# Layer 1 of a two-layer hybrid backbone: attention scores, value products and LRU gates on the whole 128x128 array

## The chip, the cores and the metric

The kernel runs on one core of one Trainium2 chip. The metric is the device time of one execution in microseconds (us). Engines are named as in the profile: PE (TensorE, matrix products), PEld (its weight loads), DVE (VectorE), ACT (ScalarE), POOL (GpSimd) and SP (SyncE, which here only issues DMAs). Each engine carries out its own list of instructions in order, and waits on semaphores for the others.

## The reference, cut to what matters

The model has two layers for 512 latent tokens and 256 context tokens. The change lies in the token mixing of layer 1, which has an RG-LRU over 512 channels and a neighbourhood attention of 8 heads of 64 channels.

```python
def rglru(u_pre, gate_pre, conv_w, conv_b, gate_w, gate_b, lam, h0):
    u = conv(u_pre) + conv_b
    gates = jnp.einsum('btnc,zgncd->btzgnd', u.reshape(B, T, LRU_BLOCKS, LRU_BW), gate_w)   # 8 blocks of 64 x 64
    gates = jax.nn.sigmoid((gates.reshape(B, T, 2, 2, W) + gate_b).astype(jnp.float32))
    rg, ig = gates[:, :, :, 0], gates[:, :, :, 1]
    log_a = -LRU_C * rg * jax.nn.softplus(-lam.astype(jnp.float32))
    a = jnp.exp(log_a)
    xin = jnp.sqrt(-jnp.expm1(2 * log_a)) * ig * u[:, :, None, :]
    _, h = lax.associative_scan(_linear_combine, (a, xin), axis=time)      # z = 0 forwards, z = 1 backwards
    y = h[0] + jnp.flip(h[1], 1)
    return y.astype(u_pre.dtype) * jax.nn.gelu(gate_pre), h[:, :, -1]
```

The attention takes, for each head and each block of 16 columns of the 8 x 64 grid, the scores of 128 queries against 256 local and 256 context keys, adds a bias and a mask to the local ones, and multiplies the softmax with the values. After the mixing come the output projection, a gated residual add, and an MLP.

## The kernel before, in words

Everything is held with channels on partitions and tokens along the free dimension. A dense product is made by `gemm`: a weight tile `w` comes by DMA on SP's queue, ACT casts its high part `wh`, POOL (at times DVE) subtracts the low part `wl`, and PE makes `wh*xh + wh*xl + wl*xh` into a PSUM tile `psg` of 128 x 512; such operands are of the type fp32r. Products of plain f32 operands are called by `mm` too; each of them has two records in the trace.

Layer 1's mixing runs over i = 0 to 3, each time `na(i)` (two heads of the attention, on partitions 0 to 63 and 64 to 127) and `lru(i)` (128 channels, which are two blocks of 64). The code is written in that order; a scheduler then sets the order of every engine's list, so products of `lru(i)` stand between those of `na(i)` and of `na(i+1)`.

- `na(p)`: three tiles of the input projection give the queries `qn`, keys `kl` and values. For each column block n and each head q, scores go to `pss` (2 buffers), DVE adds the bias `mb` and takes the maximum, ACT makes the exponential `sl` with its sum, DVE normalizes it, PE transposes it to `pst`, ACT copies that to `pT`, and PE makes the value product `pso` (1 buffer). The results gather in `ax`, which `split_x` turns into the high and low parts `yh`, `yl` of rows 2p+1.
- `lru(i)`: two tiles of the input projection, a convolution to `u`, then for each direction z and gate g the gate products to `psl` (1 buffer) for 256 and for 512 tokens, and their tanh on ACT. Behind the gates of a direction: Exp to `a`, a tanh, the square of `a` on POOL (`a2`), two products on DVE, Sqrt on ACT, a product on POOL, the scans on DVE (256 and 512 tokens). The sum of both directions is multiplied by the gelu branch on POOL and split into rows 2i of `yh`, `yl`.
- Tiles of the same `tag` in the pool `pl` share one buffer: `a0` and `a1` hold `a` of the two directions, `a2` the square and, earlier, the gelu's work tile.

After the four iterations `out_proj(1, 0, res, Y, 0, 6, ...)` makes 8 tiles from rows 0 to 5 of `yh`, `yl` (so it needs `lru(0)` to `lru(2)` and `na(0)` to `na(2)`), and `out_halves` makes the part of rows 6 and 7 (`lru(3)` and `na(3)`), for 256 tokens at a time. The MLP follows.

Of the kernel before, what the change touches and what calls it, by code (L numbers as in the profile page):

```python
# [117 lines left out]
def hybrid_kernel(ctx: ExitStack, tc: tile.TileContext, A, out):  # L118
# [36 lines left out]
    # conditioning: modulation columns of half the channels for pairs of indices, a generator over weight tiles  # L155
# [33 lines left out]
    def ada_first(q, pa, psa, tag):  # L189
        """Shift and scale of the first norm for a quarter of the channels."""  # L190
        ps = psa.tile([P, P], F32, tag=tag, name=nm("psada"))
        for k in range(NK):
            if k % 2 == 0:
                w = pa.tile([P, 2, 512], F32, tag="adaw", name=nm("adaw"))
                nc.sync.dma_start(w, A["ada_0"][q, k // 2])
            for j in range(4):
                mm(ps[32 * j:32 * j + 32, :], sc[:, k, :], w[:, k % 2, P * j:P * j + P], k == 0, k == NK - 1)
        rows = pa.tile([P, P], F32, tag="rows", name=nm("rows"), bufs=1)
        nc.vector.tensor_copy(rows, ps)
        pt = psa.tile([P, P], F32, tag=tag, name=nm("pst"))  # L200
        nc.tensor.transpose(pt, rows, ident)
        src = pt.rearrange("p (i t r) -> p i t r", i=2, t=2)
        for i in range(2):
            o = 8 * i + 2 * q
            bias = cols[:, COLS["ada_b"][0] + o:COLS["ada_b"][0] + o + 2]
            for cnd in range(2):
                nc.vector.scalar_tensor_tensor(mod[:, 0, o:o + 2, cnd], src[:, i, :, cnd], float(i), bias, op0=ALU.add, op1=ALU.add)
# [11 lines left out]
    def split_w(ap, both, pool=None):  # L219
        """High and low part of a weight tile; the low part takes turns between GpSimd and VectorE where both are free."""  # L220
        m = ap.shape[1]
        n = m if pool else D
        pool = pool or (wide[0] if wcount[0] % 3 == 2 else None) or wp
        wpool = wide[0] if wide[0] is not None and pool is wide[0] else wp
        w = wpool.tile([P, D], F32, tag="w", bufs=3 if wpool is wp else None, name=nm("w"))[:, 0:m]
        nc.sync.dma_start(w, ap)
        wh = pool.tile([P, n], F32R, tag="wh", name=nm("wh"))[:, 0:m]
        nc.scalar.copy(wh, w)  # L228
        wl = pool.tile([P, n], F32R, tag="wl", name=nm("wl"))[:, 0:m]
        wcount[0] += 1  # L230
        eng = nc.vector if (2, 0, 3, 1)[wcount[0] % 4] < both else nc.gpsimd
        eng.tensor_tensor(wl, w, wh.bitcast(F32), op=ALU.subtract)  # L232
        return wh, wl

    def gemm(ap, xs, psp, both=0, k0=0, k1=NK, x0=0):
        """One output tile [P, n] for each (high, low, n) in xs, three single-pass products per contraction tile."""
        w = split_w(ap[:, P * k0:P * k1], both)
        res = [gemm_w(w, x, psp, x0) for x in xs]
        for _ in range(bg[1]):
            next(bg[0], None)  # L240
        return res
# [12 lines left out]
    def halves(x):  # L254
        """The two halves of the tokens of an operand or a residual."""
        n = x[2] if isinstance(x, tuple) else x.shape[2]
        sl = (slice(0, n // 2), slice(n // 2, n))
        return [(x[0][:, :, a], x[1][:, :, a], n // 2) for a in sl] if isinstance(x, tuple) else [x[:, :, a] for a in sl]

    def gemm_group(ws, ps, xs):  # L260
        """Several output tiles with the contraction outermost, for an input that is still being made."""
        for k in range(NK):
            for (wh, wl), row in zip(ws, ps):
                for (xh, xl, _), p_ in zip(xs, row):
                    for a, (w, x_) in enumerate(((wh, xh), (wh, xl), (wl, xh))):
                        mm(p_, w[:, P * k:P * k + P], x_[:, k, :], k == 0 and a == 0, k == NK - 1 and a == 2)
# [5 lines left out]
    class Stats:  # L272
        """Sums of squares of every token, gathered tile by tile, and 1/rms on every partition."""
# [55 lines left out]
    def out_proj(layer, cnd, res, x, k0, k1, psp, both, stats=None, x0=None):  # L329
        """Part of the contraction of an output projection, a generator over weight tiles (yields their time on TensorE)."""  # L330
        for m in range(NK):
            add_gated(res[:, m, :], gemm(A["out_w"][layer, m], [x], psp, both, k0, k1, k0 if x0 is None else x0)[0], cnd, m, layer, 2)
            if stats:
                stats.add(res[:, m, :])
            yield x[2] / 512 * 0.65 * (k1 - k0)

    def out_halves(layer, res, x, k0, ws, psp, stats):
        """The last part of an output projection for one half of the tokens after the other."""
# [6 lines left out]
    def mlp(layer, cnd, n, res, FC, psp, side, both, rb, G, stats=None, done=None):  # L345
        us = n / 512 * 5.2
        with ExitStack() as st:
# [39 lines left out]
            if done:  # L387
                # the end by halves of the tokens, so that the first leaves while the second is made
# [8 lines left out]
    # ================= layer 0: modulated norm =================  # L397
# [37 lines left out]
    # derived per-channel columns  # L435
# [29 lines left out]
    # scratch in DRAM  # L465
# [104 lines left out]
    def mlstm_head(h):  # L570
# [32 lines left out]
        # scores, shared by both directions  # L603
# [204 lines left out]
    # ================= RWKV: chunked recurrence, both directions in step =================  # L808
# [4 lines left out]
    def add_set():  # L813
        """Tiles of every other chunk."""
        sets.append(st_r.enter_context(tc.tile_pool(name=f"set{len(sets)}", bufs=1)))
# [12 lines left out]
    def pre(s, X):  # L828
        """Everything of a chunk that does not need the state."""
# [23 lines left out]
        # inverses of the 16 x 16 diagonal blocks, one per partition  # L853
# [14 lines left out]
        # the keys by token  # L868
# [20 lines left out]
        # merge to 32 x 32 blocks, one per group of 32 partitions  # L889
# [19 lines left out]
        # merge to 64 x 64: only the block off the diagonal is new  # L909
# [69 lines left out]
    def rwkv_norm(y):  # L979
        """Head norm of some chunks [P, groups, chunks x pairs, 64], in place."""  # L980
# [13 lines left out]
    def rwkv_norms(s):  # L994
        """Head norm of the chunks that are complete after a step."""
# [6 lines left out]
    def rwkv_gate(si, dst, po, psp):  # L1002
        """Bonus and gate of a stream; dst(pair) is their place."""
# [11 lines left out]
    # ================= work that fills TensorE beside the recurrence =================  # L1015
# [3 lines left out]
    def lat_mlstm(res):  # L1019
        """The mLSTM part of the latents' output projection."""  # L1020
# [11 lines left out]
    def ctx_mlstm():  # L1032
        """The mLSTM part of the context's output projection."""
# [31 lines left out]
    def pull(gen, us):  # L1065
        """Emit units of gen worth us more microseconds of TensorE."""
# [74 lines left out]
    # ================= layer 0: latents =================  # L1141
# [34 lines left out]
    # ================= layer 1 =================  # L1176
# [23 lines left out]
    gw = pl.tile([P, 2, 2, 4, 64], F32, name="gw")  # L1200
    nc.scalar.dma_start(gw, A["gate_w"])
# [6 lines left out]
    def lru(i):  # L1208
# [21 lines left out]
        AA, XX = [], []  # L1230
        for z in range(2):
            th = []
            for g_ in range(2):
                t_ = pl.tile([P, T], F32, tag=f"t{g_}{z}", name=nm("th"))
                for off, n, _ in SEGS:
                    pq = psm.tile([P, n], F32, tag="l", name=nm("psl"))
                    for q in range(2):
                        mm(pq[hs_[q], :], gw[hs_[q], z, g_, i, :], u_[hs_[q], off:off + n])
                    nc.scalar.activation(t_[:, off:off + n], pq, AF.Tanh,
                                         bias=DV["lgb"][:, 8 * z + 4 * g_ + i:8 * z + 4 * g_ + i + 1], scale=0.5)  # L1240
                th.append(t_)
            tr, ti = th
# [32 lines left out]
    def na(p):  # L1275
        qn = pl2.tile([P, NB, 8, 16], F32, tag="qn", name=nm("qn"))
        pq, = gemm(A["od_in"][8 + p], XL, psg4)
        nc.scalar.activation(qn.rearrange("p n r c -> p r n c")[:, ::-1, :, ::-1], pq.rearrange("p (r n c) -> p r n c", r=8, n=NB),
                             AF.Copy, scale=0.125)
# [17 lines left out]
        # bias of the window, and what lies outside of it  # L1297
# [12 lines left out]
        ax = pl.tile([P, LT], F32, tag="ax", name=nm("ax"))  # L1310
        for n in range(NB):
            po_ = psm.tile([P, P], F32, tag="o", name=nm("pso"))
            for q in range(2):
                ps = psm.tile([P, 512], F32, tag="s", bufs=2, name=nm("pss"))
                qs = qn[hs_[q], n].rearrange("p r c -> p (r c)")
                s3 = ps[:, 0:256].rearrange("p (r c) -> p r c", r=8)
                mm(s3, qs, kl[hs_[q]].rearrange("p (r c) -> p r c", r=8)[:, :, BAND[n]:BAND[n] + 32])
                mm(ps[:, 256:512], qs, kc[hs_[q], :])
# [12 lines left out]
                for j in range(4):  # L1331
                    jv = 2 * n + j if j < 2 else 6 + j
                    mm(po_[hs_[q], :], vt_[:, jv, hs_[q]], pT[:, j, :], j == 0, j == 3)
            nc.vector.tensor_copy(ax.rearrange("p (r n c) -> p r n c", r=8, n=NB)[:, :, n, :],
                                  po_.rearrange("p (r c) -> p r c", r=8)[:, ::-1, ::-1])
        split_x(yh[:, 2 * p + 1, :], yl[:, 2 * p + 1, :], ax)
# [48 lines left out]
def _ktile(w, mt):  # L1385
    """[K, M] -> [M/mt][128][K/128 * mt], each tile's rows contiguous."""
# [83 lines left out]
```

## Time and profile before

| | us |
|---|---|
| three runs | 2079.46, 2080.81, 2088.39 |
| median | 2080.81 |
| span of the profiled execution, first to last instruction | 2084.8 |
| PE busy in the span | 1973.1 (95%) |
| mean granted clock of PE | 0.971 |

The profiled execution is one more execution of the program; of it the span is known, and no time around it is listed. The 95% are an average over stages. Matmuls are pipelined and a record's end is modelled, so a record of 0.39 us can have its successor 0.23 us behind it: what a matmul costs is read from the distance between starts. The stage of the change lasts from 1430.82 us (first query product of `na(0)`) to 1694.09 us (first product of `out_halves`).

### The profile page before, as it was taken

How to read it: one execution, taken by the hardware profiler on the slowest of the kernel's cores; microseconds unless marked ns; L12 is line 12 of the kernel's file. 1: busy time of each engine (PE TensorE's matmuls, PEld its weight loads, DVE VectorE, ACT ScalarE, POOL GpSimd, SP SyncE). 2: the span in 40 equal slices, each digit the busy share in tenths (PEclk: the TensorE clock that was granted, in tenths of full speed). 3: DMA queues.
4: the chain of work that ended last, by engine and by line, in shares of the span. 5: the costliest groups of instructions: out<-in, count | busy, mean ns of one | idle time of the engine just before them, and what ended most of it. 6: DMA issues, size and time to landing. Idle time of an engine off the chain costs nothing. (4 is left out here: it accounts for less than half of the span.)

```text
span 2084.8 us, 36853 instructions
## 1 busy us (share of the span) xinstructions
PE 1973.1 (95%) x14924; PEld 1599.6 (77%) x14924; DVE 1084.0 (52%) x2087; ACT 874.0 (42%) x1441; POOL 833.9 (40%) x561
## 2 busy tenths in 40 slices
PE   6999998889887999999999999999999999999998
PEld 4787776667676889888588888888666687888887
DVE  6754545767868666776551221253666663122122
ACT  5443445445533444443342332443665644233232
POOL 1455545233322222223144444435454454444444
PEclk9999999999888999999999999999999999999999
DMA  8355657554585555444633233335211122332332
GB/s 319 96 176 200 208 195 228 147 154 116 162 236 147 131 160 160 135 133 163 198 88 104 92 102 93 90 109 154 61 51 33 56 74 82 100 98 94 91 96 77
DMA packets 177595, 271.63 MB, mean 130 GB/s; under 512 B 75601, under 2 KB 114129, under 8 KB 177425
## 3 DMA queue, kind: packets, MB, share of 16 engines
q1 hardware_dynamic: 172368, 263.76, 42.0%
q10 hardware_dynamic: 5056, 5.51, 0.8%
q8 instruction: 118, 1.93, 0.4%
q14 instruction: 53, 0.43, 0.1%
HBM read 244.06 MB, written 25.17 MB: 129 GB/s over the span
## 5 line engine op out<-in xcount | busy, mean ns | idle before, releaser
L232 POOL TENSOR_TENSOR wl<-w,wh 128x1024 fp32r<-128x1024 f32 (+3 forms) x252 | 575.6, 2287 | 872.8 <-PE psg L134 425.2
L228 ACT CAST wh<-w 128x1024 fp32r<-128x1024 f32 (+3 forms) x319 | 313.5, 985 | 544.8 <-PE psg L134 463.2
L134 PE MATMUL psg<-xh,wh 128*128 128x512 f32 (+1 forms) x1440 | 503.2, 364 | 15.6 <-DVE k L699 3.1
L134 PE MATMUL psg<-xl,wh 128*128 128x512 f32 (+1 forms) x1440 | 502.1, 360 | 0.6 <-DVE xl L324 0.3
L134 PEld LDWEIGHTS psg<-xh,wh 128*128 128x128 f32 x1440 | 274.6, 192 | 76.9 <-issue 24.4
L134 PE MATMUL psg<-xh,wl 128*128 128x512 f32 (+1 forms) x1440 | 329.6, 359 | 0.0
L134 PEld LDWEIGHTS psg<-xl,wh 128*128 128x128 f32 x1440 | 276.4, 192 | 51.0 <-issue 10.2
L134 PEld LDWEIGHTS psg<-xh,wl 128*128 128x128 f32 x1440 | 242.7, 191 | 45.9 <-issue 10.5
L134 PE MATMUL psg<-hh,wh 128*128 128x512 f32 (+1 forms) x800 | 268.2, 352 | 3.7 <-DVE r L372 1.9
L134 PE MATMUL psg<-hl,wh 128*128 128x512 f32 (+1 forms) x800 | 270.8, 352 | 0.9 <-DVE hl L270 0.9
L327 DVE SCALAR_TENSOR_TENSOR res_l<-psg,mod,res_l 128x512 f32<-128x512 f32 (+1 forms) x108 | 74.3, 689 | 282.5 <-PE psg L134 282.4
L134 PEld LDWEIGHTS psg<-hh,wh 128*128 128x128 f32 x800 | 152.0, 190 | 25.6 <-DVE r L372 2.2
L134 PEld LDWEIGHTS psg<-hl,wh 128*128 128x128 f32 x800 | 152.3, 190 | 22.6 <-DVE hl L270 1.3
L134 PE MATMUL psg<-hh,wl 128*128 128x512 f32 (+1 forms) x800 | 166.0, 349 | 0.0
L134 PEld LDWEIGHTS psg<-hh,wl 128*128 128x128 f32 x800 | 131.7, 189 | 20.5
L372 DVE TENSOR_SCALAR r<-psg 128x512 f32<-128x512 f32 (+1 forms) x96 | 57.4, 599 | 171.0 <-PE psg L134 170.9
L270 DVE TENSOR_TENSOR hl<-r,hh 128x512 fp32r<-128x512 f32 (+1 forms) x96 | 88.1, 921 | 85.7 <-ACT hh L269 85.6
L373 ACT ACTIVATE r<-r 128x512 f32<-128x512 f32 (+1 forms) x96 | 53.5, 559 | 120.9 <-DVE r L372 120.9
L232 DVE TENSOR_TENSOR wl<-w,wh 128x1024 fp32r<-128x1024 f32 (+1 forms) x67 | 83.3, 1243 | 27.6 <-ACT wh L228 18.2
L134 PE MATMUL psada<-adaw,sc 128*32 128x256 f32 (+1 forms) x896 | 69.2, 378 | 12.4 <-DMA adaw<-in_ada_w_dram 6.8
L878 DVE TENSOR_TENSOR tm<-M,Xi 64x15 f32<-64x15 f32 (+4 forms) x180 | 63.9, 355 | 17.9 <-DMA M<-dA 14.4
L269 ACT CAST hh<-r 128x512 fp32r<-128x512 f32 (+1 forms) x96 | 52.6, 550 | 2.9
(418 smaller groups left out, 2852.8 us busy)
## 6 DMA issues: line engine op xcount, KB each, us to landing
w<-in_w_dram SPq DMA_DIRECT2D x192, 512.0 KB, 3.7
adaw<-in_ada_w_dram SPq DMA_DIRECT2D x80, 512.0 KB, 4.9
w<-in_ev_in_dram SPq DMA_DIRECT2D x47, 512.0 KB, 4.0
w<-in_od_in_dram SPq DMA_DIRECT2D x32, 512.0 KB, 3.7
adaw<-in_ada_dram SPq DMA_DIRECT2D x16, 512.0 KB, 11.4
w<-in_out_w_dram SPq DMA_DIRECT2D x32, 256.0 KB, 2.9
bk<-bkD SPq DMA_DIRECT2D x12, 512.0 KB, 4.5
ar<-arD SPq DMA_DIRECT2D x12, 512.0 KB, 4.7
```

Of the source, the lines that this page charges most:

```text
L134: return nc.tensor.matmul(o, l, r, start=start, stop=stop, skip_group_check=shared, **kw)
L228: nc.scalar.copy(wh, w)
L232: eng.tensor_tensor(wl, w, wh.bitcast(F32), op=ALU.subtract)
L269: nc.scalar.copy(h, x)
L270: nc.vector.tensor_tensor(l, x, h.bitcast(F32), op=ALU.subtract)
L327: nc.vector.scalar_tensor_tensor(r_, ps, modcol(layer, idx, m, cnd), r_, op0=ALU.mult, op1=ALU.add)
L372: nc.vector.tensor_scalar(r_, ps, 0.0, None, op0=ALU.max)
L373: nc.scalar.activation(r_, r_, AF.Square)
L878: nc.vector.tensor_tensor(t_, M[:, m:16, j:j + 1].to_broadcast([64, n, m]), Xi[:, j:j + 1, 0:m].to_broadcast([64, n, m]), op=ALU.mult)
```

## The change

Three groups of products that used 64 rows or 64 columns of the array use all 128 x 128 of it.

- Scores: the queries of each head go into their own tile `qz[:, q]`, whose other 64 partitions are zero, and the product contracts over all 128 partitions of `kl` and of `kc`. `qz` is one buffer, zeroed once by POOL, where `qn` had two; ACT fills it in two instructions for two heads.
- Value products: all 128 columns of the values are multiplied with each head's `pT`, and the half that belongs to the head is read from `pso`. The tile `ax` is gone: ACT casts `yh` and DVE makes `yl` from `pso` directly, for each block and head apart (64 x 128 each).
- Gates: the two 64 x 64 blocks stand on the diagonal of a zeroed 128 x 128 weight. Weights and `u` are split into fp32r parts `gwh`, `gwl`, `uh`, `ul`, and each gate is three fp32r products. The weights come by two DMAs on ACT's queue in each `lru`. `uh` and `ul` take the buffers `a0` and `a1`. All eight gate products of an `lru` are written ahead of both directions' further work.

```diff
-    gw = pl.tile([P, 2, 2, 4, 64], F32, name="gw")
-    nc.scalar.dma_start(gw, A["gate_w"])
+    gw = pl.tile([P, 4, P], F32, name="gw")
+    gwh = pl.tile([P, 4, P], F32R, name="gwh")
+    gwl = pl.tile([P, 4, P], F32R, name="gwl")
+    nc.gpsimd.memset(gw, 0.0)
...
+    qz = pl.tile([P, 2, GW // 16, 8, 16], F32, name="qz")
+    nc.gpsimd.memset(qz, 0.0)
...
-        AA, XX = [], []
...
+        for q in range(2):
+            nc.scalar.dma_start(gw[hs_[q], :, hs_[q]].rearrange("p (z g) c -> p z g c", z=2), A["gate_w"][hs_[q], :, :, i, :])
+        nc.scalar.copy(gwh, gw)
+        nc.gpsimd.tensor_tensor(gwl, gw, gwh.bitcast(F32), op=ALU.subtract)
+        uh = pl.tile([P, T], F32R, tag="a0", name=nm("uh"))
+        ul = pl.tile([P, T], F32R, tag="a1", name=nm("ul"))
+        split_x(uh, ul, u_)
+        TH = []
         for z in range(2):
-            th = []
             for g_ in range(2):
                 t_ = pl.tile([P, T], F32, tag=f"t{g_}{z}", name=nm("th"))
                 for off, n, _ in SEGS:
                     pq = psm.tile([P, n], F32, tag="l", name=nm("psl"))
-                    for q in range(2):
-                        mm(pq[hs_[q], :], gw[hs_[q], z, g_, i, :], u_[hs_[q], off:off + n])
+                    for a, (w, x) in enumerate(((gwh, uh), (gwh, ul), (gwl, uh))):
+                        mm(pq, w[:, 2 * z + g_, :], x[:, off:off + n], a == 0, a == 2)
                     nc.scalar.activation(t_[:, off:off + n], pq, AF.Tanh,
                                          bias=DV["lgb"][:, 8 * z + 4 * g_ + i:8 * z + 4 * g_ + i + 1], scale=0.5)
-                th.append(t_)
-            tr, ti = th
+                TH.append(t_)
+        AA, XX = [], []
+        for z in range(2):
+            tr, ti = TH[2 * z:2 * z + 2]
...
-        qn = pl2.tile([P, NB, 8, 16], F32, tag="qn", name=nm("qn"))
         pq, = gemm(A["od_in"][8 + p], XL, psg4)
...
+        for q in range(2):
+            nc.scalar.activation(qz[hs_[q], q].rearrange("p n r c -> p r n c")[:, ::-1, :, ::-1],
+                                 pq[hs_[q]].rearrange("p (r n c) -> p r n c", r=8, n=NB), AF.Copy, scale=0.125)
...
-                qs = qn[hs_[q], n].rearrange("p r c -> p (r c)")
+                qs = qz[:, q, n].rearrange("p r c -> p (r c)")
                 s3 = ps[:, 0:256].rearrange("p (r c) -> p r c", r=8)
-                mm(s3, qs, kl[hs_[q]].rearrange("p (r c) -> p r c", r=8)[:, :, BAND[n]:BAND[n] + 32])
-                mm(ps[:, 256:512], qs, kc[hs_[q], :])
+                mm(s3, qs, kl.rearrange("p (r c) -> p r c", r=8)[:, :, BAND[n]:BAND[n] + 32])
+                mm(ps[:, 256:512], qs, kc)
...
-                    mm(po_[hs_[q], :], vt_[:, jv, hs_[q]], pT[:, j, :], j == 0, j == 3)
-            nc.vector.tensor_copy(ax.rearrange("p (r n c) -> p r n c", r=8, n=NB)[:, :, n, :],
-                                  po_.rearrange("p (r c) -> p r c", r=8)[:, ::-1, ::-1])
-        split_x(yh[:, 2 * p + 1, :], yl[:, 2 * p + 1, :], ax)
+                    mm(po_[:, q, :], vt_[:, jv, :], pT[:, j, :], j == 0, j == 3)
+                src = po_[hs_[q], q].rearrange("p (r c) -> p r c", r=8)[:, ::-1, ::-1]
+                h_, l_ = (y[hs_[q], 2 * p + 1].rearrange("p (r n c) -> p r n c", r=8, n=NB)[:, :, n, :] for y in (yh, yl))
+                nc.scalar.copy(h_, src)
+                nc.vector.tensor_tensor(l_, src, h_.bitcast(F32), op=ALU.subtract)
```

The scheduler makes new lists from this. Three places of them show what moves. In the names, `psl_` numbers rise with the order in which the gate products are written; tiles `psg_16885` and above are those of the output projection.

PE's list of before, where the last `lru` begins (its first gate product is `psl_16795`) and the output projection starts (`psg_16889`):

```order
L134 MATMUL psl_16783<-u_16720,gw 64x512 x2
L1328 MATMUL pst_16652<-cst,sl_16648 128x128 x4
L134 MATMUL pso_16597<-pT_16634,vt_16479 64x128 x4
L1328 MATMUL pst_16673<-cst,sl_16669 128x128 x4
L134 MATMUL psl_16795<-u_16720,gw 64x256 x2
L134 MATMUL pso_16641<-pT_16657,vt_16479 64x128 x4
L134 MATMUL psg_16889<-yh_14998,wh_16885 128x512
L134 MATMUL psg_16889<-yl_14999,wh_16885 128x512
```

PE's list of the change at the corresponding place, from the last gate product of `lru(2)` (`psl_16425`) to the first of `lru(3)` (`psl_16866`); eight products of the output projection stand in it, of which two are shown:

```order
L134 MATMUL psl_16425<-uh_16382,gwh 128x512
L134 MATMUL psl_16425<-ul_16383,gwh 128x512
L134 MATMUL psl_16425<-uh_16382,gwl 128x512
L134 MATMUL pso_16681<-pT_16697,vt_16558 128x128 x4
L1341 MATMUL pst_16762<-cst,sl_16758 128x128 x4
L134 MATMUL psg_16993<-yh_14998,wh_16989 128x512
L134 MATMUL psg_16993<-yl_14999,wh_16989 128x512
...
L134 MATMUL pso_16681<-pT_16720,vt_16558 128x128 x4
L134 MATMUL pso_16728<-pT_16744,vt_16558 128x128 x4
L134 MATMUL pso_16728<-pT_16767,vt_16558 128x128 x4
L134 MATMUL psl_16866<-uh_16861,gwh 128x256
L134 MATMUL psl_16866<-ul_16862,gwh 128x256
```

Before, five of the eight gate products of `lru(3)` (`psl_16770` to `psl_16795`) stood ahead of the output projection, and the projection's first tile ran on through rows 0 to 5 without a break. Now all eight stand behind its first eight products, which cover rows 0 to 3; row 4 is the output of `lru(2)`.

The last gate product of `lru(3)` in PE's list of before, inside the fourth tile of the output projection; four and five sixths of its eight tiles, 87 products, follow before the first one of `out_halves` (`psg_17115`):

```order
L134 MATMUL psg_16967<-yh_14998,wh_16963 128x512
L134 MATMUL psl_16808<-u_16720,gw 64x512 x2
L134 MATMUL psg_16967<-yl_14999,wh_16963 128x512
...
L134 MATMUL psg_17071<-yh_14998,wl_17069 128x512 x6
L134 MATMUL psg_17115<-yh_14998,wh_16837 128x256
```

The same place in the change (`psg_17175` is the last tile of the output projection, `psg_17219` and `psg_17229` the first two of `out_halves`):

```order
L134 MATMUL psl_16899<-uh_16861,gwh 128x256
L134 MATMUL psl_16899<-ul_16862,gwh 128x256
L134 MATMUL psl_16899<-uh_16861,gwl 128x256
L134 MATMUL psg_17175<-yh_14998,wl_17173 128x512 x4
L134 MATMUL psl_16904<-uh_16861,gwh 128x512
L134 MATMUL psl_16904<-ul_16862,gwh 128x512
L134 MATMUL psl_16904<-uh_16861,gwl 128x512
L134 MATMUL psg_17219<-yh_14998,wh_16941 128x256
L134 MATMUL psg_17229<-yh_14998,wh_16947 128x256
L134 MATMUL psg_17219<-yl_14999,wh_16941 128x256
```

The 87 products between the last gate product and `out_halves` have become none.

ACT's list of the change behind the last two gate products, up to the cast of `lru(3)`'s output that `out_halves` reads (`th_16865`, `th_16876` are the tanhs of direction 0, `th_16887`, `th_16898` of direction 1):

```order
L1251 ACTIVATE th_16898<-psl_16899,der 128x256
L1259 ACTIVATE a_16916<-th_16887,der 128x768
L1251 ACTIVATE th_16898<-psl_16904,der 128x512
L1259 ACTIVATE a_16909<-th_16865,der 128x768
L1260 ACTIVATE th_16887<-th_16887,der 128x768
L1260 ACTIVATE th_16865<-th_16865,der 128x768
L1268 ACT_TABLE_LOAD
L1268 ACTIVATE th_16865<-th_16865 128x768
L1268 ACTIVATE th_16887<-th_16887 128x768
L269 CAST yh_14998<-th_16876 128x512
```

And ACT's list of before, from the first gate's second part (direction 1) on:

```order
L1239 ACTIVATE th_16794<-psl_16799,der 128x512
L1245 ACTIVATE a_16812<-th_16794,der 128x768
L1246 ACTIVATE th_16794<-th_16794,der 128x768
L228 CAST wh_16963<-w_16961 128x768
L1239 ACTIVATE th_16803<-psl_16804,der 128x256
L1254 ACT_TABLE_LOAD
L1254 ACTIVATE th_16794<-th_16794 128x768
L228 CAST wh_16989<-w_16987 128x768
L1239 ACT_TABLE_LOAD
L1239 ACTIVATE th_16803<-psl_16808,der 128x512
```

Before, only the tanh of the last gate stood behind the last gate product; direction 0 and the Exp, tanh and Sqrt of direction 1 were done. Now Exp, tanh and Sqrt of both directions stand behind it: `a_16909` and `a_16916` are written into the buffers from which `psl_16904` still reads `uh` and `ul`.

## Rows read from the trace of the kernel before

**Rows 1.** The page, part 1: busy us, share, instructions.

```profile
PE 1973.1 (95%) x14924; PEld 1599.6 (77%) x14924; DVE 1084.0 (52%) x2087; ACT 874.0 (42%) x1441; POOL 833.9 (40%) x561
```

**Rows 2.** Windows of the stage: engines' busy us (records), PE's clock, DMA.

```profile
1430.82:1655.20 224.38, 223.40 (x1134) 152.50 (x1133) 139.10 (x233) 132.82 (x224) 102.36 (x71) 1.00 0.18 55
1430.82:1694.09 263.27, 262.29 (x1306) 181.70 (x1305) 161.68 (x253) 153.53 (x248) 130.84 (x85) 1.00 0.21 63
```

**Rows 3.** Waits of PE, 1431 to 1720 us: total, times, longest.

```profile
PE psl L134 <- ACT th L1239: 1.0, 2, 0.5
```

**Rows 4.** Timeline of PE: start, length, instruction, records; tile shapes alternate.

```profile
1464.06 0.70 PE L134 MATMUL pss<-kl,qn 64*128 64x256 f32 x2
1464.69 0.66 PE L1328 MATMUL pst<-cst,sl 128*128 128x128 f32 x4
1465.27 0.70 PE L134 MATMUL pss<-ukv,qn 64*128 64x256 f32 x2
...
1466.79 1.08 PE L134 MATMUL psl<-u,gw 64*64 64x512 f32 x4
1467.80 0.50 PE L134 MATMUL psg<-xh,wh 128*128 128x512 f32 x1
...
1475.24 0.65 PE L134 MATMUL psl<-u,gw 64*64 64x256 f32 x4
1475.82 0.50 PE L134 MATMUL psg<-xl,wh 128*128 128x512 f32 x1
```

**Rows 5.** Timeline of PE where all tiles are 128x128.

```profile
1632.10 0.39 PE L134 MATMUL psg<-xh,wh 128*128 128x512 f32 x1
1632.33 0.60 PE L1328 MATMUL pst<-cst,sl 128*128 128x128 f32 x4
...
1633.00 0.39 PE L134 MATMUL psg<-xh,wh 128*128 128x512 f32 x1
...
1677.29 0.39 PE L134 MATMUL psg<-yh,wh 128*128 128x512 f32 x1
...
1681.49 0.39 PE L134 MATMUL psg<-yh,wh 128*128 128x512 f32 x1
```

**Rows 6.** Lines by form, PEld, 1400 to 1760 us: busy us, mean ns, idle before.

```profile
L1328 PEld LDWEIGHTS pst<-cst,sl 128*128 128x128 f32 x128 | 14.5, 140 | 7.4 <-issue 3.8 <-DVE sl L1325 0.8 <-DVE ax L1334 0.4
```

**Rows 7.** Timeline of ACT, DVE and POOL behind the last gate product.

```profile
1675.92 0.69 ACT L1239 ACTIVATE th<-psl,der 128x512 f32<-128x512 f32 x1
...
1677.68 1.85 POOL L1258 TENSOR_TENSOR th<-th,th 128x768 f32<-128x768 f32 x1 [1.15 <-DVE th L1250]
...
1679.56 2.31 DVE L1263 TENSOR_TENSOR_SCAN th<-a,th 128x256 f32<-128x256 f32 x1 [1.30 <-POOL th L1258]
...
1681.91 1.28 DVE L1263 TENSOR_TENSOR_SCAN th<-a,th,th 128x512 f32<-128x512 f32 x1
...
1684.00 1.29 POOL L1268 TENSOR_TENSOR th<-th,gl 128x512 f32<-128x512 f32 x1 [2.67 <-DVE th L1267]
...
1685.32 0.62 ACT L269 CAST yh<-th 128x512 fp32r<-128x512 f32 x1 [4.16 <-POOL th L1268]
...
1685.98 1.67 DVE L270 TENSOR_TENSOR yl<-th,yh 128x512 fp32r<-128x512 f32 x1 [1.40 <-ACT yh L269]
```

**Rows 8.** Lines by form, ACT, 1430 to 1694 us.

```profile
L1254 ACT ACT_TABLE_LOAD x8 | 10.3, 1283 | 0.1
L1245 ACT ACTIVATE a<-th,der 128x768 f32<-128x768 f32 x8 | 8.3, 1034 | 0.1
L1254 ACT ACTIVATE th<-th 128x768 f32<-128x768 f32 x8 | 6.8, 846 | 3.7 <-DVE th L1249 3.7
```

**Rows 9.** Windows around a wait of PE ahead of the stage.

```profile
1416.00:1418.70 2.70, 0.54 (x5) 0.33 (x3) 0.00 (x0) 1.07 (x2) 2.24 (x5) 1.00 0.57 209
1419.70:1423.10 3.40, 3.33 (x17) 3.04 (x16) 2.07 (x1) 1.05 (x1) 2.33 (x2) 0.50 0.40 101
1423.10:1426.00 2.90, 2.90 (x26) 2.90 (x26) 0.00 (x0) 0.17 (x1) 2.25 (x1) 1.00 0.88 326
```

More of the change, by code (lines that the diff above doesn't have):

```diff
@@ L1275, in na @@
     def na(p):
-        qn = pl2.tile([P, NB, 8, 16], F32, tag="qn", name=nm("qn"))
         pq, = gemm(A["od_in"][8 + p], XL, psg4)
-        nc.scalar.activation(qn.rearrange("p n r c -> p r n c")[:, ::-1, :, ::-1], pq.rearrange("p (r n c) -> p r n c", r=8, n=NB),
-                             AF.Copy, scale=0.125)
+        for q in range(2):
+            nc.scalar.activation(qz[hs_[q], q].rearrange("p n r c -> p r n c")[:, ::-1, :, ::-1],
+                                 pq[hs_[q]].rearrange("p (r n c) -> p r n c", r=8, n=NB), AF.Copy, scale=0.125)
         kl = pl2.tile([P, LT], F32, tag="kl", name=nm("kl"))
@@ L1309, in na @@
             MB.append(mb)
-        ax = pl.tile([P, LT], F32, tag="ax", name=nm("ax"))
         for n in range(NB):
-            po_ = psm.tile([P, P], F32, tag="o", name=nm("pso"))
+            po_ = psm.tile([P, 2, P], F32, tag="o", name=nm("pso"))
             for q in range(2):
                 ps = psm.tile([P, 512], F32, tag="s", bufs=2, name=nm("pss"))
-                qs = qn[hs_[q], n].rearrange("p r c -> p (r c)")
+                qs = qz[:, q, n].rearrange("p r c -> p (r c)")
                 s3 = ps[:, 0:256].rearrange("p (r c) -> p r c", r=8)
-                mm(s3, qs, kl[hs_[q]].rearrange("p (r c) -> p r c", r=8)[:, :, BAND[n]:BAND[n] + 32])
-                mm(ps[:, 256:512], qs, kc[hs_[q], :])
+                mm(s3, qs, kl.rearrange("p (r c) -> p r c", r=8)[:, :, BAND[n]:BAND[n] + 32])
+                mm(ps[:, 256:512], qs, kc)
                 nc.vector.tensor_tensor(s3, s3, MB[q][:, (0, 1, 1, 2)[n]], op=ALU.add)
```

## Prediction

> **What bounds the kernel now.** I read the shares of the engines first, then the windows of the stage, then the waits inside it, and last the distances between PE's instructions. On the page PE is busy for 95% of the span and nothing else for more than 77% [rows 1]; that is a mean over stages, so the stage itself counts. From 1430.82 to 1694.09 us, which is 263.27 us, PE is busy for 262.29 us at the full clock (1.00), ACT for 153.53 and DVE for 161.68 [rows 2]. The reader is to see that PE bounds this stage almost alone: the waits that the trace names inside it come to 1.0 us [rows 3]. So a microsecond taken out of PE's work here comes off the end, and a microsecond that PE is made to wait goes on it.
>
> But busy is not streaming. Where all tiles are 128x128, the start of one fp32r product of 512 columns follows that of another 0.233 us behind (18 in 1677.29 to 1681.49), and four transposes of 128 columns take 0.90 − 2 × 0.233 = 0.43 us, or 0.109 each (1632.10 to 1633.00, two products and four transposes) [rows 5]. Where shapes alternate, the distances are longer [rows 4]. Two records of a score product (256 columns) take 0.63 us. Four transposes between scores take 0.58. A gate's group takes 1.01 us with 512 columns and 0.58 with 256: 256 more columns cost 0.43, which for four records of two halves that run side by side is 0.215 per record. By that the score pair streams for 0.43 of its 0.63 us, and the four transposes for 0.44 of 0.58.
>
> The sum of streaming over the stage: 624 `psg` products × 0.233 = 145.6; 168 transposes × 0.109 = 18.3; 256 records of `pso` (128 columns) × 0.109 = 27.9; 128 of `pss` × 0.215 = 27.5; gates 16 × 0.86 + 16 × 0.43 = 20.6. That is 239.9 us. Of the 263.3 us, less 1.0 of waits, 22.4 remain, and PE's list has 164 places in the stage where the tile's shape changes: **0.137 us for each change of shape**, which the 0.20 around a score pair (in and out) and the 0.14 around four transposes bear out.
>
> **The change on PE: a gain of 26.2 us.** In the new list every tile of the stage is 128x128, so no change of shape is left: −22.4. Score and value products keep their counts and columns. The gates become three fp32r products: 16 × 3 × (0.233 + 0.117) = 16.8 for 20.6: −3.8. Bounds: the change of shape could cost as little as the 0.14 seen around four transposes for an in and an out together (0.07 each, −11.5), or as much as 0.20 for a score's in and out with the rest spread otherwise (0.10 each, −16.4); but then some 6 to 11 us of the stage would have no owner, and I keep −26.2 with −15 as the far end.
>
> One rule speaks against it. In the trace the two heads' scores stand apart, with transposes or gates between [rows 4], so they have nothing to lose by filling the array; value products of neighbouring heads may overlap a little, and that is inside the measured stage. The Trainium skill (TensorEngine Tiling (Array Packing), When to Use Tiling) advises the reverse of this change: a contraction of 64 is to be tiled into two row groups for twice the rate. By that rule, had score pairs run side by side before, the change would double 13.75 us of them; the rows show that they did not, so the sum keeps zero.
>
> **What the change makes PE wait for.** `uh` and `ul` take the buffers of `a`. Inside one `lru`, no Exp can write `a` before the last gate product has read `uh` or `ul`; and the next `lru` cannot cast `uh`, `ul` before the scans have read `a`. Before, direction 0 went through Exp to scan while direction 1's gates were still being made, and gates read `u` itself.
>
> *End of the stage.* Before, 87 products, 20 us at 0.233, lay between the last gate product and `out_halves`, and hid the chain from 1675.92 (tanh) to 1687.65 (end of `yl`) [rows 7]. Now none lies there, and both Exp, both tanh and both Sqrt are in the chain too. From rows: last tanh 0.69 [rows 7]; of `a` and the tanh behind it three that follow, 3 × 1.03; table load 1.28; first Sqrt 0.85 [rows 8]; POOL's two products 2 × 1.85, one behind the other; the second direction's scans 2.31 + 1.28; sum 0.69 (an estimate from the gap between scan and POOL's start); POOL 1.29; `yh` 0.62 [rows 7]: 15.8. `out_halves` starts with two products of 256 columns that need `yh` alone, and the third needs `yl`: 1.67 − 0.23 = 1.4 more. With 0.3 for hand-overs: **+17.5**, bounds 12 (the 11.7 us that the shorter chain of before took) and 20. Nothing covers it: the MLP needs the whole sum.
>
> *From lru(2) to lru(3).* Behind the last gate product of `lru(2)` PE has four groups of value products, four transposes and eight products of the projection, 5 × 0.44 + 8 × 0.233 = 4.1 us, and then stands at a gate product of `lru(3)`, with the rest of the projection queued behind it on PE. That gate needs `uh` and `ul`, so the chain up to the scans, without the sum and POOL's last product but with `ul` over 768 tokens (1.5 × 1.67 = 2.5): 0.69 + 3 × 1.03 + 1.28 + 0.85 + 3.70 + 3.59 + 2.5 = 15.7. In ACT's list seven other instructions stand inside it (weight casts, `pT`, `yh` by blocks); at ACT's mean of 0.62 us (153.53 over 248) [rows 2] that is 4.3, part of which falls into waits for DVE: about 19. Less 4.1: **+15**, bounds 10 and 19.
>
> *The two earlier hand-overs* have the same chain of some 20 us, but PE's list has 19.4 us (lru(0) to lru(1)) and 23.4 us of work (lru(1) to lru(2)) between, by the durations above: **+3**, bounds 0 and 8.
>
> *Ahead of it.* The gates' weights now come through ACT's queue in each `lru`, and their cast on ACT waits for the landing, with weight casts queued behind; POOL clears `qz` (1024 columns) and `gw` (512) ahead of its weight subtractions, at two POOL products of 768 columns no more than 3.7 us. PE waits ahead of the stage already: between 1416.00 and 1418.70 it is busy for 0.54 of 2.70 us [rows 9]. **+2.5**, bounds 0 and 5. The smaller edits (two Activations for `qz`, `yh` and `yl` by blocks: eight more instructions on ACT and three on DVE in each `na`) lie under PE: ACT is busy for 58% of the stage.
>
> *The clock.* After the wait just named the granted clock is 0.50, the 1.2 GHz level, from 1419.70 to 1423.10: 17 records take 3.40 us, where at 1.00 26 take 2.90 [rows 9]. The difference is 17 × (0.200 − 0.112) = 1.5 us. Two long waits and perhaps two short ones cost 3 to 6: **+4**, bounds 2 and 7.
>
> *Taken away:* the 1.0 us of waits for the one `psl` buffer partly goes: **−1**.
>
> **The sum:** −26.2 + 17.5 + 15 + 3 + 2.5 + 4 − 1 = +14.8 us. The profiled span is 2084.8, which becomes 2099.6. The median of the three runs, 2080.81, is 4 us below that execution; I put the sum on the median: **2095.6, say 2095 us**. A measurement of this kernel can tell about 0.5%, 10.4 us, from no change.
>
> **Rivals.**
> *The drains win (other side).* The waits that I price from the longest chain are covered by the other engine work, because `lru` i+1 is not needed until late and chains are shorter than the means say. If waits and clock together stay under 16 us, the kernel is faster by over 10.4 us; with none, 2080.8 − 26.2 = 2054.6. For it: rows 2 give PE's slack engines 100 us. Against: 87 products have become none at the end of the stage, and there alone the shortest chain is 12 us. Likely place if true: about 2068. Chance 0.10.
> *A draw.* Gain and waits cancel within 10.4 us, about 2081: this needs each of the two long waits near its lower bound (12 and 10, sum +5) or the gain at its full size and no cost for head and clock. Chance 0.30.
> *The forecast*, slower by over 10.4 us: 0.58, its own range 2091 to 2112.
> *Whole-array loads don't overlap.* Score and gate products that used 64 rows would wait for their weights: 128 + 96 loads of 0.140 us [rows 6] are 31 us, and the time 2095 + 31 = 2126. Four transposes that each load a whole tile stand 0.109 us apart [rows 5], shorter than a load and a pass together, which speaks against it. The Trainium skill (TensorE: Matmul & The Clock Gate, Part 3, What overlaps and what doesn't) has a load overlap running products only where the row group differs, which would make this case; on the rows above the trace does not agree. Chance 0.02.
>
> The slower cases hold 0.60, the draw 0.30, the faster ones 0.10. The range from 2072 to 2112 reaches into the draw's whole width and to the sum of the upper bounds without the rare loads (17.5 + 19 + 6 + 4 + 6 − 26 = +26.5, about 2107, and a little for a smaller gain).
>
> **What the profile of the changed kernel would show.** Right: no long distances at PE's shape changes (four transposes between scores 0.44, not 0.58); one idle stretch of PE of 12 to 20 us directly ahead of `out_halves`, whose chain of waits goes back through `yh`, POOL, the scans, Sqrt and Exp to the last gate's tanh; a second of 10 to 19 us ahead of the first gate product of `lru(3)`, released by `ul` on DVE; a granted clock of 0.50 behind each. Wrong: if these two together are under 16 us, or if PE's busy time in the stage falls by less than 15 us, or if idle stretches at the hand-overs of `lru(0)` and `lru(1)` are over 8 us each.

## The result and the profile after

The changed kernel takes 2107.66 us (median of 4 runs, 2104.69 to 2116.44) where the kernel before takes 2080.14 (4 runs): the ratio is 1.0134, 95% interval 1.011 to 1.0157. It is slower by 27.5 us; +14.8 was forecast, and the time lies inside the forecast range.

The page's first part, to be laid beside [rows 1], shows PE with less work and a longer span:

```profile
span 2108.3 us, 36874 instructions
...
PE 1960.3 (93%) x14892; PEld 1628.9 (77%) x14892; DVE 1093.5 (52%) x2103; ACT 877.7 (42%) x1475; POOL 842.3 (40%) x567
```

The windows of the changed kernel: the whole stage (first query product of `na(0)` to the first product of `out_halves`), then two pieces of it. Columns: length, busy us (records) of PE, PEld, DVE, ACT and POOL, PE's granted clock, DMA share, GB/s.

```profile
1425.28:1717.69 292.41, 247.28 (x1275) 208.37 (x1273) 168.93 (x271) 157.25 (x281) 138.04 (x88) 0.92 0.19 61
1639.05:1666.36 27.31, 14.43 (x43) 10.81 (x42) 18.45 (x24) 10.84 (x18) 12.16 (x8) 0.50 0.09 29
1703.91:1717.69 13.78, 0.00 (x1) 0.00 (x1) 8.07 (x8) 3.78 (x5) 7.05 (x4) 0.50 0.01 3
```

Against [rows 2] the stage is 292.41 − 263.27 = 29.1 us longer. What follows it takes 390.7 us before and 390.6 after in the profiled executions, and what lies ahead of it is 5.5 us shorter after, so the loss is all here. PE is idle for 292.41 − 247.28 = 45.1 us where it was for 1.0. The reader is to see the clock as well: 0.50 for 27.31 us on end, although PE was busy for 14.43 us of them.

PE's waits in the stage (total, times, longest), where [rows 3] had one line of 1.0 us:

```profile
PE psg L134 <- ACT yh L269: 18.8, 2, 17.8
PE pso L134 <- DVE yl L1350: 8.9, 6, 3.6
PE psl L134 <- ACT uh L269: 3.9, 1, 3.9
PE psl L134 <- DVE ul L270: 2.9, 1, 2.9
PE pss L134 <- ACT sl L1336: 2.8, 1, 2.8
PE psg L134 <- DVE kl L1297: 2.5, 1, 2.5
PE psg L134 <- ACT wh L228: 2.3, 1, 2.3
PE psg L134 <- ACT qz L1292: 1.4, 1, 1.4
```

The largest stands ahead of `out_halves`. The chain that ended last shows what PE waited for there (start, length, what; pieces of "issue", each of 0.09 us or less, are left out between the lines):

```profile
1699.74 1.03 ACT a L1259
1700.77 0.57 ACT th L1251
1701.35 0.92 ACT a L1259
1702.26 1.85 ACT th L1260 x2
1704.21 0.97 DVE th L1263
1705.25 1.48 POOL a L1262
1706.75 2.55 DVE th L1263
1709.32 0.85 ACT th L1268
1710.24 2.57 POOL th L1272
1712.84 0.70 DVE th L1277
1713.57 1.29 DVE th L1277
1714.89 0.70 DVE th L1281
1715.72 1.27 POOL th L1282
1717.02 0.63 ACT yh L269
```

From the first Exp, which waits for the last gate products, to `yh` nothing lies beside it on PE. In [rows 7] the same chain began at the last gate's tanh and lay under 20 us of the projection.

### The profile page after: what moved, and what is told of

Same layout as the page of the kernel before. It is cut to its first block, busy times and chain, and to the rows that moved or that the text cites. A ratio compares the mean times of both kernels' runs of the same rounds, so it can differ in the third digit from the quotient of the medians.

```text
span 2108.3 us, 36874 instructions
## 1 busy us (share of the span) xinstructions
PE 1960.3 (93%) x14892; PEld 1628.9 (77%) x14892; DVE 1093.5 (52%) x2103; ACT 877.7 (42%) x1475; POOL 842.3 (40%) x567
## 3 DMA queue, kind: packets, MB, share of 16 engines
q1 hardware_dynamic: 172368, 263.76, 40.5%
## 4 chain that ended last, share of the span: by engine, by line
PE 53%; DVE 11%; DMA 5%; issue 2%; ACT 2%; POOL 1%; SPq 1%; DVEq 0%; POOLq 0%; ACTq 0%
PE psg L134 46%; DVE tm L878 2%; DVE Xi L880 1%; DMA Xr<-invD 1%; PE psA L134 1%; PE psC L134 1%; PE pso L134 1%; DVE wl L232 1%; PE pss L134 1%; DVE u L1224 1%; DMA invD<-Xi 1%; DMA dA<-AB 1%; PE psI L134 1%; DMA M<-dA 1%; SPq L883 1%
## 5 line engine op out<-in xcount | busy, mean ns | idle before, releaser
L134 PEld LDWEIGHTS psg<-hl,wh 128*128 128x128 f32 x800 | 151.2, 189 | 22.6 <-DVE hl L270 1.3
L232 DVE TENSOR_TENSOR wl<-w,wh 128x1024 fp32r<-128x1024 f32 (+1 forms) x67 | 83.0, 1239 | 27.5 <-ACT wh L228 15.5
```

Source lines behind the costliest of these rows:

```text
L134: return nc.tensor.matmul(o, l, r, start=start, stop=stop, skip_group_check=shared, **kw)
```

## The experiments

A run's time on the chip scatters by 5 us and more, and in the profiles the stage starts anywhere between 1420 and 1435 us. The ratios are those to the kernel before, run beside each experiment. Each run is also read by the window of its own stage: length, and PE's work, which is its busy time less half of what of it lay in stretches at clock 0.50. Before, length and work are 263.3 and 262.3 us; in the changed kernel 292.4 and 238.4 (of its 247.3 us, 14.4 and, from 1523.00 to 1526.41, 3.4 were at 0.50).

**E1. Whole-array scores and values, but plain f32 gates on `u`.** The gates keep their block-diagonal weight, without `uh`, `ul` and the split weights, and each direction's Exp stands right behind its gates again. Buffers, split and order go together here; E4 takes the buffers alone.

```diff
-                    for a, (w, x) in enumerate(((gwh, uh), (gwh, ul), (gwl, uh))):
-                        mm(pq, w[:, 2 * z + g_, :], x[:, off:off + n], a == 0, a == 2)
+                    mm(pq, gw[:, 2 * z + g_, :], u_[:, off:off + n])
```

> The changed kernel with whole-array scores and value products, but each gate as one plain f32 product of the block-diagonal weight with u itself, and each direction's Exp right behind its gates as before: no uh, ul, no split weights. Theory 1 (the lost time is the lru's new chain: uh and ul in the buffers of a, all gates ahead): no change of tile shape is left, -22.4 us, 72 products lie between the last gate and out_halves, some 4 us of waits of the value products remain: about 2062 us, PE's wait ahead of out_halves under 2 us. Theory 2 (the waits come from the casts by block, pso held by two engines, one qz): about 20 us of waits and clock stay, 2080. Theory 3 (whole-array products themselves are slow, their loads are not overlapped): 2095 or more.

Measured: 2075.88 us, ratio 0.9955 (0.9936 to 0.9973). The wait ahead of `out_halves` is gone and the waits at the hand-overs nearly; 11.1 us of idle time stay, 6.1 of them for `yl`, and 6.8 us at clock 0.50:

```profile
1425.50:1682.20 256.70, 245.58 (x1243) 201.29 (x1241) 162.47 (x265) 157.36 (x279) 130.17 (x85) 0.99 0.21 64
```

Theory 1 holds for the lru's chain: without it the kernel is 32 us faster than the changed one by the medians. But against the kernel before the gain is half of what was expected: 11.1 us of idle time stay, where 4 were allowed, and the clock takes another 3.3. Theory 3 is out.

**E2. The gates of before, scores and values of the change.**

```diff
-                    for a, (w, x) in enumerate(((gwh, uh), (gwh, ul), (gwl, uh))):
-                        mm(pq, w[:, 2 * z + g_, :], x[:, off:off + n], a == 0, a == 2)
+                    for q in range(2):
+                        mm(pq[hs_[q], :], gw[hs_[q], z, g_, i, :], u_[hs_[q], off:off + n])
```

> The changed kernel with the gates of the kernel before (64x64 halves, f32, u itself), so scores and value products alone are changed. The list has 68 changes of shape where before has 164. Theory 1: 96 x 0.137 = -13.1 us and some 4 us of waits: about 2072 us, 10 above the run with whole-array f32 gates. Theory 2: about 2090. Theory 3: 2095 or more.

Measured: 2081.98 us, ratio 0.9995 (0.998 to 1.001): no change that can be measured. No theory had it right.

```profile
1431.54:1693.53 261.99, 255.28 (x1307) 192.98 (x1305) 164.78 (x265) 159.26 (x279) 129.46 (x85) 1.00 0.20 62
```

Work fell by 7.0 us in place of 13.1, and 5.7 us of new idle time took most of that back. Scores and values alone bring next to nothing; why, E8 to E10 tell.

**E3. The new gates alone in the kernel before**, with `uh`, `ul` in `a0`, `a1` and all gates ahead, as in the diff.

> The kernel before with the new gates alone (block-diagonal, split, uh and ul in the buffers of a). The list has 99 changes of shape, and no product between the last gate and out_halves. Theory 1: -8.9 - 3.8 + 17.5 at the end, some 15 at the hand-overs, some 8 for the clock: about 2109 us. Theory 2: the gates alone cost nothing, about 2068.

Measured: 2115.07 us, ratio 1.0144 (1.0122 to 1.0166), with Theory 1's sign and size. PE waits ahead of the projection's rest and ahead of `out_halves`:

```profile
PE psg L134 <- ACT yh L269: 18.8, 2, 17.8
PE psl L134 <- ACT uh L269: 15.8, 1, 15.8
PE psl L134 <- DVE ul L270: 3.7, 1, 3.7
```

The gates' part of the change alone makes all of the loss, and here `uh` alone holds PE for 15.8 us at `lru(3)`.

**E4 and E5. Own buffers for `uh` and `ul`, and the control.** Both have one buffer for `kl` and for `b_`, which makes the room; E4 has the two lines for `uh` and `ul` as well.

```diff
-        uh = pl.tile([P, T], F32R, tag="a0", name=nm("uh"))
-        ul = pl.tile([P, T], F32R, tag="a1", name=nm("ul"))
+        uh = pl.tile([P, T], F32R, tag="uh", name=nm("uh"))
+        ul = pl.tile([P, T], F32R, tag="ul", name=nm("ul"))
```

> The changed kernel with buffers of their own for uh and ul (paid for by one buffer in place of two for kl and for the bias b_). 18 products, 4.2 us, now lie between the last gate and out_halves. If the shared buffers are the cause: direction 0 goes on early, the wait ahead of out_halves falls from 17.8 to 9 to 12 us, the one ahead of lru(3) from 8 to under 2, and the slow clock with them: about 2088 us. If it is the order (gates late in PE's list, whoever owns the buffers): only the 4.2 us are gained, 2100 to 2104.

> The control to the run with own buffers: the changed kernel with one buffer in place of two for kl and for the bias b_, and uh and ul still in the buffers of a. If the own buffers made the gain of 21 us: as the changed kernel, 2104 to 2112, with waits of about 17.8 us ahead of out_halves. If the smaller buffers, or the order that they bring, made it: about 2087.

Measured: E4 2086.56 us, ratio 1.0 (0.9984 to 1.0017); E5 2109.08 us, ratio 1.0132 (1.0104 to 1.016). So the two tags are worth 22 us by the medians, 27 by the ratios. E5's wait ahead of `out_halves` is 18.2 us, E4's 6.9 (9 to 12 had been expected), and none for `uh` is left. One line of E5, then E4's:

```profile
PE psg L134 <- ACT yh L269: 19.1, 2, 18.2
...
PE pst L1341 <- DVE sl L1338: 7.5, 4, 3.0
PE psg L134 <- ACT yh L269: 6.9, 1, 6.9
PE pso L134 <- DVE yl L1350: 5.1, 3, 3.7
PE psl L134 <- ACT th L1251: 1.3, 1, 1.3
PE psl L134 <- DVE ul L270: 1.0, 1, 1.0
```

Since only the tags differ, the shared buffers are the cause; that 18 products (4.2 us, of the 11.3 by which the wait fell) then come to lie behind the last gate is their consequence, not a second cause. E4's work is 237.6 us, as that of the changed kernel: fp32r gates in own buffers keep the full gain on PE and still end level with the kernel before, through 22.6 us of waits on DVE and ACT and 3.7 of clock. E4 is still slower than E1, by 11 us by the medians or 9 by the ratios. The two differ in the split of `u` and of the weights and in the order of the gates; no run takes these apart.

**E6. The changed kernel with `ax` back**, one DVE copy out of `pso` for each head and block.

```diff
-                nc.scalar.copy(h_, src)
-                nc.vector.tensor_tensor(l_, src, h_.bitcast(F32), op=ALU.subtract)
+                nc.vector.tensor_copy(ax[hs_[q]].rearrange("p (r n c) -> p r n c", r=8, n=NB)[:, :, n, :],
+                                      po_[hs_[q], q].rearrange("p (r c) -> p r c", r=8)[:, ::-1, ::-1])
```

> The changed kernel, but pso is copied to ax by one DVE instruction for each head and block, and yh and yl are made from ax as before. Theory A (PE's 8.9 us of waits for yl come from pso being held by ACT's cast and then DVE's subtraction): PE's waits for the release of pso fall under 3 us and the time to 2095 to 2101, the end's 17.8 us stay. Theory B (DVE is late for other reasons, the lru's scans): the waits stay whoever reads pso, 2105 to 2110.

Measured: 2114.07 us, ratio 1.0162 (1.0131 to 1.0192). Theory A fell, and the time is above Theory B's range too. The waits for the release of `pso` were halved (8.9 to 4.2 us), and those of the transposes for `sl`, on the same engine, rose from 0.9 to 9.3:

```profile
PE pst L1342 <- DVE sl L1339: 9.3, 5, 5.0
...
PE pso L134 <- DVE ax L1348: 4.2, 2, 3.7
```

Idle time is 47.3 us, against 45.1 in the changed kernel. DVE's timeline shows it busy with the convolution, and the copies out of `pso` between its pieces:

```profile
1635.18 1.35 DVE L1264 SCALAR_TENSOR_TENSOR th<-th,u 128x768 f32<-128x768 f32 x1
1636.57 2.31 DVE L1222 TENSOR_SCALAR u<-up,cols 128x256 f32<-128x256 f32 x2
1638.80 2.48 DVE L1224 SCALAR_TENSOR_TENSOR u<-up,cols,u 128x256 f32<-128x256 f32 x3
1641.31 0.28 DVE L1348 COPY ax<-pso 64x128 f32<-64x128 f32 x1
```

**E7. E1 with `ax`.**

> Whole-array f32 gates and ax together: scores, value products and gates are on the whole array, and the two causes of waits (the lru's buffers and pso's readers) are gone. Theory A: the 6.1 us of waits for yl and some 3 us of slow clock that the run with f32 gates still had go: 2064 to 2069 us. Theory B: as that run, 2072 to 2078 (0.9955 of before).

Measured: 2069.79 us, ratio 0.9941 (0.9918 to 0.9965). Here `ax` helps a little: waits for `pso` fall from 6.1 to 0.9 us, no stretch at 0.50 is left in the stage, and the stage is 6.6 us shorter than E1's:

```profile
1435.14:1685.29 250.15, 242.65 (x1243) 198.74 (x1241) 163.64 (x269) 153.06 (x251) 128.84 (x85) 1.00 0.22 66
```

The time is 6 us under that of E1 by the medians and 3 by the ratios, at the upper edge of Theory A; the intervals of E1 and E7 overlap, so by time alone it isn't told apart.

**E8. f32 gates on the whole array, and nothing else** (E1's line in the kernel before, with the block-diagonal `gw` loaded in each `lru`).

> The kernel before with the gates alone on the whole array, each one plain f32 product of the block-diagonal weight with u. 107 of 164 changes of shape stay. If each change of shape costs the same 0.137 us: -7.8 us, about 2073. If those to and from the 64x64 gate tiles cost some 0.2 and those of scores and values some 0.07, as the busy times of the runs before this one suggest (255.3 with old gates, 242.3 with none): -11 to -13 us, 2067 to 2070.

Measured: 2066.13 us, ratio 0.9932 (0.9908 to 0.9957), with 2.1 us of idle time:

```profile
1420.35:1673.44 253.09, 251.01 (x1239) 186.61 (x1238) 154.96 (x253) 153.04 (x248) 131.03 (x85) 1.00 0.22 67
```

Work fell by 11.3 us for 57 changes of shape, 0.20 each, as the second alternative had it (part of it is overlap, below).

**E9 and E10. E8 with whole-array scores, and E8 with whole-array values (with `ax`).** E9 adds `qz` as in the diff, E10 the lines of E6.

> The kernel before with whole-array f32 gates and whole-array scores; value products as before. 58 changes of shape stay, 49 fewer than with the gates alone. PE's work in the stage there was 251.0 us, and 242.7 with none left, so 8.4 us for 107 changes. Theory A (each of these 0.078 us): 247.2 us of work. Theory B (only scores pay, since their 64 rows change the way in which the array is filled, while 64 columns change nothing ahead of them): 243 us. Time with 2 to 5 us of waits: A 2064, B 2060, if the stage alone decides.

> The kernel before with whole-array f32 gates and whole-array value products, copied to ax for each head apart; scores as before. 66 changes of shape stay, 41 fewer than with the gates alone. Theory A (each 0.078 us): 247.8 us of work. Theory B (scores alone pay): 251 us, nothing gained, and the 16 more copies on DVE add 1 to 3 us of waits. Time: A 2064, B 2067.

Measured: E9 2071.93 us, ratio 0.9948 (0.9929 to 0.9967), work 248.3 (250.0 less half of 3.4 us at 0.50); E10 2068.86 us, ratio 0.9926 (0.9906 to 0.9947), work 249.7. Scores take 2.7 us off E8's work, values 1.3: neither theory. Their sum is less than half of what both bring together (8.4, E7). The trace explains most of it. E8's first scores:

```profile
1436.81 0.71 PE L134 MATMUL pss<-kl,qn 64*128 64x256 f32 x4
1437.35 0.60 PE L134 MATMUL pss<-ukv,qn 64*128 64x256 f32 x4
1437.88 0.50 PE L134 MATMUL psg<-xh,wh 128*128 128x512 f32 x1
```

and E9's:

```profile
1446.33 0.60 PE L134 MATMUL pss<-kl,qz 128*128 128x256 f32 x2
1446.77 0.59 PE L134 MATMUL pss<-ukv,qz 128*128 128x256 f32 x2
1447.20 0.59 PE L134 MATMUL pss<-kl,qz 128*128 128x256 f32 x2
1447.63 0.59 PE L134 MATMUL pss<-ukv,qz 128*128 128x256 f32 x2
1447.88 0.58 PE L134 MATMUL psg<-xh,wh 128*128 128x512 f32 x1
```

In E8 four records take 0.54 us, in E9 0.87: with 64 rows each, the two heads ran side by side where they stand next to each other. Counted over the stage, 26 of E8's score records (18 before) start 6 to 14 ns behind the one ahead, where 216 ns is the rule, which saves 5.3 us (3.7 before); neighbouring value products save 1.1 us more (1.5 before). Whole-array products lose this. Put back, a change of shape costs (8.4 + 6.4)/107 = 0.14 us from E8 to E7 and, since E8's overlap is 1.2 us larger than that of before, (11.3 − 1.2)/57 = 0.18 from before to E8. By the same count E9 gives (2.7 + 5.3)/49 = 0.16; E10, in whose order only 16 score records still run side by side, gives (1.3 + 2.0 + 1.1)/41 = 0.11. Why its changes are the cheapest is open.

E7 to E10 are all faster than both kernels and cannot be told apart by their times; by the stage E7 is the shortest (250.2 us) and E10 next (252.1).

## Why the prediction was right, and where it was not

The direction was right, and the two large waits were right in place and size, with the shared buffers as their cause (E4 and E5). But the loss, +27.5 us, is nearly twice the +14.8 that was forecast. Two terms lie outside their own bounds: the earlier waits (12.1 us, bounds 0 to 8) and the clock (8.9, bounds 2 to 7). The ledger of the stage, forecast against measured:

| term | forecast | measured | from |
|---|---|---|---|
| PE's work | −26.2 | −23.9 | 262.3 to 238.4 |
| wait ahead of `out_halves` | +17.5 | +17.8 | PE's waits |
| `lru(2)` to `lru(3)` | +15 | +15.2 | seven waits between 1635 and 1662 us |
| earlier waits | +3 | +12.1 | the rest of 45.1 us |
| clock | +4 | +8.9 | half of 14.4 + 3.4 us busy at 0.50 |
| ahead of the stage | +2.5 | about 0 | below |
| waits of before | −1 | −1.0 | [rows 3] |
| sum | +14.8 | +29.1 | stage; +27.5 by the medians |

- **The end of the stage.** Right in place, cause and size. The chain was not the one that I added up: I left out the square on POOL (1.48) and two products on DVE (0.97 and 2.55). I charged a table load of 1.28, which ran beside them on ACT, POOL's products at 3.70, of which 2.57 lay in the chain, DVE's scans at 3.59, which took 1.99, and `yl`, which PE did not wait for. That the errors cancelled is luck.
- **lru(2) to lru(3).** The size was right, the one releaser was not: of 15.2 us the gate's waits for `uh` and `ul` are 6.8, and no single stretch of 10 to 19 us stands there. Of the rest, 5.1 are value products that wait for `pso`, the longest (3.6) behind DVE's convolution; 2.3 a weight cast that stands behind the Exp in ACT's list; 1.0 `yh`. E3, whose value products do not stand in between, has one wait of 15.8 us for `uh` there.
- **The earlier hand-overs** are the term that was mis-sized most. I compared PE's work between the gates with the chain's length and found them nearly equal. What I passed over is what else PE needs from ACT and DVE: waits for `sl`, `yl`, `qz`, `kl` and `pT`, the longest 2.8 us, none of them for `uh` or `ul`. The sentence that the smaller edits "lie under PE" failed with it. E1, without the chain, still has 8.7 us of such waits up to 1635 us (11.1 in its stage), E2 has 6.7 in its stage, and E8, without the whole-array scores and values, 2.1. So most of the term seems to come with scores and values; how much of it the chain adds is not shown. With the new gates, E6 shows that a single reader of `pso` only moves the waits to `sl`, which comes from DVE too; without them it does help (E1 to E7: 11.1 to 7.5 us of idle time).
- **The clock.** The price of one stretch was right (1.5 us forecast, 3.41/2 = 1.7 measured), the stretches were longer: I counted single stretches like that of [rows 9], and one lasted 27.31 us through a row of waits of 0.7 to 3.9 us. The ledger puts 14.43/2 = 7.2 us down to it. But 8.6 of the 14.43 us lie ahead of the gate that waits for `uh` at 1656.61; how much of their share PE would have waited there anyway, no run shows.
- **Ahead of the stage.** PE waited 3.5 us for a weight cast where it had waited 2.2, but the span from the same earlier wait (for `rs`) to the first query product is 40.5 us in the changed kernel and 41.5 before: no loss. The span of before has one more stretch of 3.41 us at clock 0.50 in it, which hides the longer wait.
- **PE's gain.** Mis-sized by 2.3 us, and one step of it failed: that the two heads' scores "stand apart" and "have nothing to lose". The rows that I showed are such a place, but at others of the kernel before they ran side by side, four records in 0.53 us:

```profile
1448.09 0.71 PE L134 MATMUL pss<-kl,qn 64*128 64x256 f32 x4
1448.62 0.60 PE L134 MATMUL pss<-ukv,qn 64*128 64x256 f32 x4
```

The Trainium skill (TensorEngine Tiling (Array Packing), When to Use Tiling) gives a contraction of 64 two row tiles. E8 against E9 agrees: 0.54 us for four records against 0.87. The sum came out nearly right because the 22.4 us that I put down to changes of shape were already less what the overlap saved. E1 splits the gain: whole-array shapes gave 20.0 us (262.3 to 242.3) of those 22.4, the fp32r gates 3.9 (to 238.4) of the 3.8. One reading was wrong as well: a distance from start to start, as in [rows 4], holds one change of shape and not an in and an out, so its 0.20 and 0.14 us are prices of one, and the bounds of 0.07 and 0.10 were too low.

- **The range.** Its upper end was added up from 17.5, 6, 4 and 6 us where the terms' own upper bounds are 20, 8, 5 and 7; these give +33 and not +26.5. The measured +27.5 is above the sum as it was written down, and lies under 2112 us by what was added "for a smaller gain".
- **The rivals.** The drains did not win, because the waits and the clock came to 54 us and not under 16. Loads of whole-array weights cost nothing that could be seen: E9's scores follow at 0.216 us on whole tiles, each with a load of its own. That rival found no support here. The rule named beside it (the Trainium skill, TensorE: Matmul & The Clock Gate, Part 3, What overlaps and what doesn't) has a load overlap running products only where the row group differs. These rows do not agree with it.

## What to carry to other kernels

Before a new operand goes into the buffer of a later result of the same chain, follow who reads it last: here two borrowed tags put Exp, Sqrt, scans and the next `lru`'s casts one behind the other, and cost over 20 us (E4 against E5) where PE's gain was 24. When the bounding engine gets faster, price its neighbours' lists and not their busy shares: DVE and ACT were busy for 63% and 61% of E2's stage and still made its gain vanish. And look in the trace at where small products run side by side before they are padded to the whole array; the gates, whose 57 changes of shape cost nearly 0.2 us each, paid for the padding in one product (E8), while scores and values gave back over 40% of theirs (6.4 of 14.8 us).

## What had not been expected of the hardware

The granted clock stayed at 0.50 (1.2 GHz) for 27.31 us in which PE was busy for 14.43 us and none of whose waits was longer than 3.9 us, while two waits of 2.6 and 2.8 us, which ended at 1517.78 and 1522.13 us, were followed by one stretch of 3.41 us. Two score products on different row halves started 6 to 14 ns apart also with f32 operands. DVE's subtraction of 512 columns took 1.67 us in [rows 7] and 0.69 us at the same place of the changed kernel, where POOL stood idle beside it; in [rows 7] POOL was subtracting weights at the time (4.11 us from 1685.25 on). That the one slows the other is not shown.
